# Value rows of the first gathered tile multiplied in the second half of the front, pair by pair

## The chip, the cores and the metric

The kernel runs on one core of a Trainium2 chip. The metric is the time of one execution on the device in microseconds (us), taken as the median of several runs. A profiled execution of the kernel gives the trace that the views below are read from.

## The reference

One layer of an encoder over 1024 tokens of width 1024, in float32. A combined projection feeds forgetting attention (FoX, 8 heads), an RWKV-7 scan (8 heads) and two merge gates; the merged result is normed into `x1`. Then comes PEER: each token picks experts by product keys and takes rows of two tables of 16384 experts.

```python
q = (xb @ w_q).reshape(t, PEER_HEADS, 2, PEER_HALF)
s = jnp.einsum('thpd,hpkd->thpk', q, sub_keys)
top_s, top_i = lax.top_k(s, K)                      # K = 16 on each side
...
best_s, best_pos = lax.top_k(cand_s.reshape(t, PEER_HEADS, K * K), K)
idx = jnp.take_along_axis(cand_i..., best_pos, axis=-1)   # 8 x 16 = 128 experts a token
gate = jax.nn.softmax(best_s, axis=-1)
h = gelu(einsum('thkd,td->thk', u_table[idx], xb))
out = einsum('thk,thkd->td', gate * h, v_table[idx])
```

The output is `layer_norm(alpha * x1 + out)`.

## The kernel before

The 1024 tokens are eight tiles of 128. **The front** runs twice, for 512 tokens each (`hf` 0 and 1): `fox` (attention), `rwkv_half` (the scan), `merge_half` (merge, output projection, norm) and `queries` (the 16 query projections and the scores of the keys). After it, `dense_block` treats the experts in two ways. Tiles 3, 4 and 5 (`DENSE`) are multiplied with all 16384 experts: a one-hot stage builds the matrix `C` of gates in 96 steps `k` (tile `ab` in, `v` out), then a loop of 128 steps `j` takes 128 experts each (`hidden`: tile `b` from `uh`, `ul`; `values`: tile `v` from `vh`, `vl`). Tiles 0, 1, 2, 6 and 7 (`GATHERED`) fetch the rows of their own experts by indirect DMA.

Two lists of small work are dealt out beside the main line. `g.B` (class `Background`) holds `topk` of each tile and `experts_in`: 128 gathers of `u` rows for a tile on the queue of GpSimd (POOL), each followed by one multiply-and-sum on VectorE (DVE). `g.V` holds `Rows.run`: for each gathered tile 64 **V steps**. A V step takes a pair of gathered value rows (two tiles of 128 x 1024, called `vr`, or `C` where places in `C` are lent) and multiplies each with a window of coefficients (`win`, one copy on ScalarE, ACT) in four float32 products into the PSUM bank `pg`. The trace has two records for each of the four, so a V step is eight records. `Rows.prepare` loads and turns the indices of a tile (`cij`, `ve`) first; `gather` asks for a pair of rows. A tile of `g.V` ends with `yd`, its result, written to DRAM; `finals` adds it to `x1` and norms.

What is dealt out is set at build time. `mm` adds up the nominal time of every product on the main line and calls `tick` of both lists; each tick adds time x `rate` to a credit, and steps are made while there is credit. A V step costs `VCOST` = 3.0, and in the loop two steps are made at a time. The rates are `RATEP` in the front, `RATEB[0]`, `RATEV[0]` in the one-hot stage, `RATEB[1]`, `RATEV[1]` in the loop and `RATEV[2]` once the keys of tile 7 are done. PE's instructions stand in the order in which the program makes them. In `dense_block` this holds for POOL and DVE too; elsewhere a scheduler orders the other engines. Each engine runs its own list in order.

In the scan, each group of 128 channels (`unit`) is a chain of small products with VectorE between them. At the points where the chain waits (`wait(us)`) a `Filler` puts in pieces of pending projections for `us` of nominal time; what is left is made at the unit's end (`F.drain`). In `merge_half` the products are `a`, `b` and `o`, in `queries` `o`; their weights come by DMA (`wh`, `wl` from `whd`).

Before the change `Rows` is made after the front, so that the first V step of tile 0 stands in the one-hot stage. Places for rows there are seven tiles `vr` and parts of `C` that are not yet used.

Of the kernel before, what the change touches and what calls it, by code (L numbers as in the profile page):

```python
# [20 lines left out]
T = 1024  # L21
# [8 lines left out]
RATEB = (2.1, 0.46)  # L30
RATEV = (4.2, 0.52, 1.25)
# [228 lines left out]
def build(tc, nc, A, dbg=None, stop=None):  # L260
    with ExitStack() as ctx:
# [4 lines left out]
        g.V.other = g.B  # L266
# [5 lines left out]
def mm(g, o, l, r, start, stop_):  # L272
    g.pe.matmul(o, l, r, start=start, stop=stop_)  # L273
# [127 lines left out]
def body(ctx, g):  # L401
# [19 lines left out]
    g.x1d = [dram(f"x1d{t}", (128, D)) for t in range(8)]  # L421
    g.scd = [dram(f"scd{t}", (128, 2048)) for t in range(8)]
# [13 lines left out]

    g.rank = g.tk.tile([128, 16, 16], BF16, name="rank")
# [29 lines left out]
    with ExitStack() as fe:  # L467
# [3 lines left out]
        for hf, (t0, n) in enumerate(PARTS):  # L471
            g.t0, g.n, g.cols = t0, n, slice(t0, t0 + n)
            with ExitStack() as hx:
# [9 lines left out]
                fox(g, hf, g.X)  # L483
                g.B.rate = RATEP[1]
# [4 lines left out]
                if g.stop not in ("fox", "rwkv"):  # L489
                    merge_half(g, hf, yr)  # L490
                g.keys.drop(more)
# [8 lines left out]
    g.psG = ctx.enter_context(tc.tile_pool(name="psG", bufs=1, space=PSUM))  # L500
    g.vx = ctx.enter_context(tc.tile_pool(name="vx", bufs=1))
    g.spare, g.over = True, False
    g.rows = Rows(g, GATHERED)
# [12 lines left out]
def front_setup(g, fe, order):  # L516
# [28 lines left out]
    g.ck = fp.tile([128, T], F32R, name="ck")  # L545
    dve.memset(g.ck.bitcast(F32), 0.0)
# [5 lines left out]
def fox(g, hf, X):  # L552
# [5 lines left out]
    ck = g.ck  # L558
    cols = g.cols
    with ExitStack() as fx:  # L560
        P = fx.enter_context(tc.tile_pool(name="fox", bufs=1))
        csel = P.tile([128, 8, 128], F32R, name="csel")
# [28 lines left out]
        with tc.tile_pool(name="fg", bufs=1) as fg, tc.tile_pool(name="xr", bufs=2) as xr:  # L591
# [21 lines left out]
            dve.scalar_tensor_tensor(ck[32:40, cols], cc, -1.0, ck[0:8, cols].bitcast(F32), op0=OP.mult, op1=OP.subtract)  # L613
            if "c" in g.dbg:
                sp.dma_start(g.dbg["c"][:, cols], cc)
# [43 lines left out]
        def chunks(ct, e, P_, yu, su, vc):  # L659
# [26 lines left out]
            yt = sm.tile([128, n], F32, name="th", bufs=4)  # L686
# [5 lines left out]
            if e:  # L692
# [4 lines left out]
                ri = sm.tile([128, n], F32, name="th", bufs=4)[0:2, :]  # L697
# [63 lines left out]
def rwkv_half(g, hf, X, kt):  # L761
# [12 lines left out]
    with ExitStack() as fx:  # L774
# [10 lines left out]
        psJ = fx.enter_context(tc.tile_pool(name="psJ", bufs=2, space=PSUM))  # L785
        psM = fx.enter_context(tc.tile_pool(name="psM", bufs=1, space=PSUM))
        psS = fx.enter_context(tc.tile_pool(name="psS", bufs=4, space=PSUM))

        def shifted(wt, out, ti):
            ps = psJ.tile([128, n], F32, name="pj")  # L790
            yield from proj_gen(g, ps, wt, X, 0)
            a = el.tile([128, n], F32, name="tmp", bufs=3)
# [6 lines left out]
        def gate(i):  # L799
            ps = psJ.tile([128, n], F32, name="pj")  # L800
            yield from proj_gen(g, ps, GATE + i, X, 0)
            t = el.tile([128, n], F32, name="tmp", bufs=3)
# [36 lines left out]
        for ct in range(5):  # L839
            if ct < 4:  # L840
                run(shifted(RW_K + ct, kt[:, ct, :], 2 + ct))
                sq = el.tile([128, n], F32, name="tmp", bufs=3)
# [96 lines left out]
        def unit(ct):  # L939
# [3 lines left out]
            def wait(us):  # L943
                F.fill(WAIT * us)
# [136 lines left out]
        g2 = el.tile([128, 512], F32, name="tmp", bufs=3)  # L1081
# [15 lines left out]
        F.fill(GN[0])  # L1097
        sums(psn, 3, sqs[3])
# [7 lines left out]
        F.fill(GN[1])  # L1106
        for ct in range(4):
            pr = psJ.tile([128, n], F32, name="pj")
# [17 lines left out]
def merge_half(g, hf, yr):  # L1126
# [3 lines left out]
    with ExitStack() as fx:  # L1130
# [4 lines left out]
        mt = mx.enter_context(tc.tile_pool(name="mt", bufs=2))  # L1135
        nt = n // 128
# [3 lines left out]
        with tc.tile_pool(name="psg", bufs=2, space=PSUM) as ps_:  # L1140
# [10 lines left out]
            for p, b in MERGE:  # L1151
                wm = g.W.get(W_MERGE + 2 * p + b)
                for dd in range(2):
# [7 lines left out]
                    if dd == 0:  # L1161
                        g.W.ahead()
                    dve.tensor_mul(t, t, pa)
# [17 lines left out]

        def turn(tts):
            for tt in tts:
                t = slice(tt * 128, (tt + 1) * 128)
                for k in range(0, 8, 4):
                    pt = ps_.tile([128, 4, 128], F32, name=f"o{(2 * tt + k // 4) % 4}", bufs=2)
# [19 lines left out]
        for m, tts in ((0, range(nt)), (1, range(half)), (1, range(half, nt))):  # L1206
            po = {tt: ps_.tile([128, 512], F32, name=f"o{tt}", bufs=2) for tt in tts}
            for k2 in range(4):
                w = g.W.get(W_OUT + 4 * m + k2)
                for kk in range(2):  # L1210
# [5 lines left out]
                    if kk == 0:  # L1216
                        g.W.ahead()
            for tt in tts:
# [7 lines left out]
        for later in rest:  # L1226
            later()
        mx.close()
        if g.stop != "merge":
            queries(g, hf, (x1h, x1l), lambda: turn(range(half, nt)), ps_)  # L1230
# [24 lines left out]
def queries(g, hf, x1, rest, ps_):  # L1255
# [5 lines left out]
    with ExitStack() as fx:  # L1261
# [3 lines left out]
        qs = {}  # L1265

        for i in range(2):
            w = g.W.get(W_Q + i)
            qs[i] = w, ps_.tile([128, n], F32, name=f"o{i}", bufs=2)
# [623 lines left out]
```

## Time and profile before

| what | us |
|---|---|
| median of three runs (lowest, highest) | 3612.66 (3611.28, 3629.97) |
| the profiled execution | 3579.33 |
| its span, first to last instruction | 3577.5 |

Busy time over the span, from the page: TensorE (PE) 3180.9 us (89%), its weight loads 2309.7 (65%), VectorE 2253.1 (63%), GpSimd 2066.4 (58%), ScalarE 1170.8 (33%). The DMA queues moved 1133.15 MB, 317 GB/s over the span. The second half of the front ends with the last product of the scores at 1776.5 us; the one-hot stage follows and the loop starts at 2212 us.

In the views, "busy" counts instructions that compute; a line's idle time is what its engine waited just before it, with the releaser behind "<-". PEclk is the clock that TensorE was granted, as a share of the full one. A DMA share of 1.00 means that all 16 DMA engines of the core were busy throughout.

### The profile page before, as it was taken

How to read it: one execution, taken by the hardware profiler on the slowest of the kernel's cores; microseconds unless marked ns; L12 is line 12 of the kernel's file. 1: busy time of each engine (PE TensorE's matmuls, PEld its weight loads, DVE VectorE, ACT ScalarE, POOL GpSimd, SP SyncE). 2: the span in 40 equal slices, each digit the busy share in tenths (PEclk: the TensorE clock that was granted, in tenths of full speed). 3: DMA queues.
4: the chain of work that ended last, by engine and by line, in shares of the span. 5: the costliest groups of instructions: out<-in, count | busy, mean ns of one | idle time of the engine just before them, and what ended most of it. 6: DMA issues, size and time to landing. Idle time of an engine off the chain costs nothing. (4 is left out here: it accounts for less than half of the span.)

```text
span 3577.5 us, 55699 instructions
## 1 busy us (share of the span) xinstructions
PE 3180.9 (89%) x20656; PEld 2309.7 (65%) x20656; DVE 2253.1 (63%) x5118; ACT 1170.8 (33%) x2453; POOL 2066.4 (58%) x1686
## 2 busy tenths in 40 slices
PE   7899998999998878788778866999999999999997
PEld 5577776786566656567533323877777777776675
DVE  2234533338988998887489854777666767774324
ACT  3442223333432221101144423333333333333332
POOL 2032114424655555663366566888887888886773
PEclk9899998999998987889889988999999999999998
DMA  6354336886979878999889999999999999999995
GB/s 223 115 184 152 116 136 246 287 314 246 328 276 378 302 272 295 369 333 386 314 348 393 373 370 368 365 360 361 389 392 378 398 385 399 397 394 341 400 400 190
DMA packets 369377, 1133.15 MB, mean 317 GB/s; under 512 B 49744, under 2 KB 88400, under 8 KB 367312
## 3 DMA queue, kind: packets, MB, share of 16 engines
q0 software_dynamic: 184320, 671.17, 49.1%
q1 hardware_dynamic: 172672, 437.64, 33.6%
q10 hardware_dynamic: 12112, 20.78, 1.6%
q8 instruction: 162, 2.65, 0.3%
q14 instruction: 111, 0.91, 0.1%
HBM read 999.87 MB, written 129.56 MB: 316 GB/s over the span
## 5 line engine op out<-in xcount | busy, mean ns | idle before, releaser
L1429 POOL DMA_INDIRECT g<-u,eidx x566 | 693.5, 1225 | 455.1 <-DVE hh L1435 160.9
L1435 DVE CUSTOM_DVE_ANT_0 g<-g,ext 128x1024 f32<-128x1024 f32 x566 | 723.6, 1288 | 75.3 <-DMA g<-u,eidx 75.1
L1731 POOL DMA_INDIRECT vr<-v,ve x434 | 459.8, 1059 | 187.6 <-issue 97.2
L291 POOL TENSOR_TENSOR wl<-wraw,wh 128x1024 fp32r<-128x1024 f32 x65 | 156.6, 2410 | 452.2 <-ACT wh L290 386.4
L273 PE MATMUL pg<-vr,win 128*32 128x512 f32 x1736 | 324.5, 630 | 76.1 <-DMA vr<-v,ve 76.0
L273 PE MATMUL b<-xh,uh 128*128 128x384 f32 x1024 | 349.9, 342 | 11.7 <-DVE C L1616 10.5
L273 PE MATMUL b<-xh,ul 128*128 128x384 f32 x1024 | 351.4, 343 | 5.1 <-POOL ul L291 4.9
L273 PE MATMUL b<-xl,uh 128*128 128x384 f32 x1024 | 349.0, 341 | 0.0
L273 PE MATMUL v<-vl,ch 128*128 128x512 f32 x768 | 304.7, 397 | 12.2 <-POOL vl L291 12.2
L273 PE MATMUL v<-vh,ch 128*128 128x512 f32 x768 | 302.5, 394 | 0.0
L273 PE MATMUL pj<-xh,wh 128*128 128x512 f32 x624 | 284.6, 456 | 20.1 <-DVE ql L586 8.6
L273 PE MATMUL v<-vh,cl 128*128 128x512 f32 x768 | 300.8, 392 | 0.0
L290 ACT CAST uh<-uraw 128x512 fp32r<-128x512 f32 x256 | 158.6, 620 | 362.6 <-PE b L273 334.6
L273 PE MATMUL pj<-xl,wh 128*128 128x512 f32 x624 | 260.3, 417 | 3.2 <-DVE xl L291 3.2
L273 PE MATMUL pj<-xh,wl 128*128 128x512 f32 x624 | 258.3, 414 | 0.0
L1731 POOL DMA_INDIRECT C<-v,ve x206 | 209.9, 1019 | 79.4 <-issue 50.5
L291 DVE TENSOR_TENSOR vl<-vraw,vh 128x512 fp32r<-128x512 f32 x128 | 134.3, 1049 | 183.8 <-ACT vh L290 175.2
L290 ACT CAST vh<-vraw 128x512 fp32r<-128x512 f32 x256 | 158.6, 621 | 257.8 <-PE v L273 214.9
L291 POOL TENSOR_TENSOR ul<-uraw,uh 128x512 fp32r<-128x512 f32 x128 | 170.6, 1333 | 85.7 <-ACT uh L290 75.8
L273 PEld LDWEIGHTS b<-xh,uh 128*128 128x128 f32 x1024 | 193.8, 189 | 32.7 <-DVE C L1616 12.6
L273 PEld LDWEIGHTS b<-xh,ul 128*128 128x128 f32 x1024 | 193.7, 189 | 32.2 <-issue 25.1
L273 PEld LDWEIGHTS b<-xl,uh 128*128 128x128 f32 x1024 | 193.9, 189 | 14.5 <-issue 10.1
(357 smaller groups left out, 6535.2 us busy)
## 6 DMA issues: line engine op xcount, KB each, us to landing
uraw<-ut SPq DMA_DIRECT2D x128, 512.0 KB, 6.7
vraw<-vt SPq DMA_DIRECT2D x128, 512.0 KB, 6.8
wraw<-w SPq DMA_DIRECT2D x75, 512.0 KB, 4.3
wh<-whd SPq DMA_DIRECT2D x75, 512.0 KB, 6.8
wl<-whd SPq DMA_DIRECT2D x75, 512.0 KB, 9.7
whd<-wh SPq DMA_DIRECT2D x71, 512.0 KB, 2.6
whd<-wl SPq DMA_DIRECT2D x71, 512.0 KB, 5.8
cd<-S SPq DMA_DIRECT2D x12, 1344.0 KB, 7.3
```

What stands on the lines that cost most here:

```text
L273: g.pe.matmul(o, l, r, start=start, stop=stop_)
L290: g.act.copy(hi, src)
L291: (lo_eng or g.dve).tensor_sub(lo, src, hi.bitcast(F32))
L1429: pool.indirect_dma_start(out=place, out_offset=None, in_=A["u"], in_offset=bass.IndirectOffsetOnAxis(ap=idx[:, n:n + 1], axis=0))
L1435: dve.tensor_tensor_reduce(out=gg, in0=gg, in1=xt, scale=1.0, scalar=0.0, op0=OP.mult, op1=OP.add, accum_out=hh[:, k:k + 1])
L1731: g.pool.indirect_dma_start(out=place, out_offset=None, in_=g.A["v"], in_offset=bass.IndirectOffsetOnAxis(ap=self.meta[i][1][:, t:t + 1], ...
```

## The change

`Rows` is made in the second half of the front, after `fox`. A V step becomes a method (`step`), and a new method `front` makes at most one thing each time it is called: a piece of `prepare`, a V step (when its rows were asked for at least 10 us ago and the last step is at least `gap` behind, both in nominal PE time), or one `gather` of a pair. It is called at the waits of a unit, twice behind the units, and in `merge_half` and `queries` behind each group of products. A step made in a unit takes 1.45 us off the filler of that wait. Rows have two places in the scan, two more in the merge and eight more in the queries; `leave` makes the steps that still hold a place before it goes. Steps made here do not tick the other lists.

To make room, `pg` takes a PSUM bank from the start of the second half's scan: there the projections share five banks `s` with the chain (before: four `s` and two `pj`), and bank `o3` of merge and queries has one buffer in place of two. The buffers `tmp` of the second half are two in place of three, `ck` is no longer kept across the halves but written to DRAM (`ckd`) and loaded again, and three small tiles of `fox` have buffers of their own. The rates change: `RATEB` from (2.1, 0.46) to (2.1, 0.575, 0.45, 0.45), `RATEV` from (4.2, 0.52, 1.25) to (3.7, 0.46, 0.44, 1.12); the third and fourth count from the end of the keys of tile 6 and of tile 7.

```diff
-RATEB = (2.1, 0.46)
-RATEV = (4.2, 0.52, 1.25)
+RATEB = (2.1, 0.575, 0.45, 0.45)
+RATEV = (3.7, 0.46, 0.44, 1.12)
+FRONT, MERGED, QUERIED = 2, 2, 8
+LAG, GAP, REST = 10.0, (14.0, 16.0), 3.0
...
 def mm(g, o, l, r, start, stop_):
...
+    g.now += us
     g.V.tick(us)
...
                 fox(g, hf, g.X)
+                if hf:
+                    g.psG = ctx.enter_context(tc.tile_pool(name="psG", bufs=1, space=PSUM))
+                    vp = hx.enter_context(tc.tile_pool(name="vf", bufs=1))
+                    g.vf = [vp.tile([128, D], F32, name=f"vr{i}") for i in range(FRONT)]
+                    g.rows = Rows(g, GATHERED)
+                    g.rows.places.add(g.vf)
...
-    g.rows = Rows(g, GATHERED)
     g.rows.places.add([g.vx.tile([128, D], F32, name=f"vr{i}") for i in range(RING)])
     g.V.add(g.rows.run())
...
-        psJ = fx.enter_context(tc.tile_pool(name="psJ", bufs=2, space=PSUM))
         psM = fx.enter_context(tc.tile_pool(name="psM", bufs=1, space=PSUM))
-        psS = fx.enter_context(tc.tile_pool(name="psS", bufs=4, space=PSUM))
+        psS = fx.enter_context(tc.tile_pool(name="psS", bufs=5 if hf else 4, space=PSUM))
+        psJ = psS if hf else fx.enter_context(tc.tile_pool(name="psJ", bufs=2, space=PSUM))
...
             def wait(us):
+                if hf and us >= 1.0:
+                    us -= g.rows.front(GAP[0])
                 F.fill(WAIT * us)
...
         F.fill(GN[0])
+        if hf:
+            g.rows.front(GAP[0])
...
                     if dd == 0:
                         g.W.ahead()
+                    if hf:
+                        g.rows.front(GAP[1])
                     dve.tensor_mul(t, t, pa)
...
                 act.copy(q[:, i % 4, :], ps)
+                if qv:
+                    g.rows.front(GAP[1])
...
-        if f"g{GATHERED[-1]}" in g.B.done:
-            g.V.rate = RATEV[2]
+        for i, t in enumerate(GATHERED[-2:]):
+            if f"g{t}" in g.B.done:
+                g.B.rate, g.V.rate = RATEB[2 + i], RATEV[2 + i]
...
+    def front(self, gap):
+        g = self.g
+        if self.prep:
+            if next(self.prep, 1):
+                self.prep = None
+        elif 0 not in self.meta:
+            if f"g{self.tiles[0]}" in g.B.done:
+                self.prep = self.prepare(0)
+                next(self.prep)
+        elif self.asked and g.now - self.asked[0] >= LAG and g.now - self.last >= gap:
+            self.asked.pop(0)
+            g.V.busy = True
+            self.step()
+            g.V.busy = False
+            self.last = g.now
+            return 1.45
+        elif self.ng < 128 and self.places.room(2) and g.now - self.last >= REST:
+            self.gather()
+            self.asked.append(g.now)
+        return 0.0
```

`step` is the body of the old loop of `run`, unchanged: one copy into `win`, four products into `pg`, and at the end of 32 pairs the result's copy and its two stores.

More of the change, by code (lines that the diff above doesn't have):

```diff
@@ L265, in build @@
         g.B, g.V = Background(tc), Background(tc)
-        g.V.other = g.B
+        g.V.other, g.now, g.rows = g.B, 0.0, None
         g.mx = ctx.enter_context(ExitStack())
@@ L490, in body @@
                     merge_half(g, hf, yr)
+                if hf and not g.stop:
+                    g.rows.leave(g.vf)
                 g.keys.drop(more)
@@ L1135, in merge_half @@
         mt = mx.enter_context(tc.tile_pool(name="mt", bufs=2))
+        mvs = []
+        if hf:
+            mv = mx.enter_context(tc.tile_pool(name="mv", bufs=1))
+            mvs = [mv.tile([128, D], F32, name=f"vr{i}") for i in range(MERGED)]
+            g.rows.places.add(mvs)
         nt = n // 128
@@ L1206, in merge_half @@
         for m, tts in ((0, range(nt)), (1, range(half)), (1, range(half, nt))):
-            po = {tt: ps_.tile([128, 512], F32, name=f"o{tt}", bufs=2) for tt in tts}
+            po = {tt: ps_.tile([128, 512], F32, name=f"o{tt}", bufs=nbuf(tt)) for tt in tts}
+            if mvs and tts.start:
+                g.rows.places.drop(mvs)
             for k2 in range(4):
@@ L1227, in merge_half @@
             later()
+        if mvs and not g.stop:
+            g.rows.leave(mvs)
         mx.close()
         if g.stop != "merge":
-            queries(g, hf, (x1h, x1l), lambda: turn(range(half, nt)), ps_)
+            queries(g, hf, (x1h, x1l), lambda: turn(range(half, nt)), ps_, nbuf)
 def layer_norm(g, mt, z):
@@ L1265, in queries @@
         qs = {}
+        qv = []
+        if hf and not g.stop:
+            qv = [qp.tile([128, D], F32, name=f"vr{i}") for i in range(QUERIED)]
+            g.rows.places.add(qv)
         for i in range(2):
             w = g.W.get(W_Q + i)
-            qs[i] = w, ps_.tile([128, n], F32, name=f"o{i}", bufs=2)
+            qs[i] = w, ps_.tile([128, n], F32, name=f"o{i}", bufs=nbuf(i))
             proj_part(g, qs[i][1][:, 0:h], w, x1, slice(0, h))
@@ L1286, in queries @@
             q = qp.tile([128, 4, n], F32, name="q", bufs=2)
+            if qv and gr == 3:
+                g.rows.places.drop(qv + g.vf)
             for i in range(4 * gr, 4 * gr + 4):
@@ L1300, in queries @@
         scores(*last)
+        if qv:
+            g.rows.leave(qv)
         for tt in range(n // 128):
@@ L1780, in leave @@
         while any(a is p for a in self.alive + self.held for p in places):
-            self.g.V._step()
+            if self.g.V.q:
+                self.g.V._step()
+            elif self.prep:
+                if next(self.prep, 1):
+                    self.prep = None
+            else:
+                self.asked.pop(0)
+                self.step()
+                self.last = self.g.now
         self.g.V.busy = False
```

117 lines of the change are left out of this document (69 added, 48 removed).

## The prediction

> **What bounds the kernel now.** First the page: the slices of TensorE, its clock and the DMA engines, and the queue of the gathers.
>
> ```profile
> PE   7899998999998878788778866999999999999997
> ...
> DMA  6354336886979878999889999999999999999995
> ...
> q0 software_dynamic: 184320, 671.17, 49.1%
> ```
>
> PE is busy without a break from the 26th slice on (the loop) and less so in the second half and the one-hot stage before it; the DMA engines stand at 8 or 9 tenths from the 17th slice to the end. q0 carries the 1280 gathers of rows (five tiles x 128, of `u` and of `v`): 671.17/1280 = 0.524 MB each, so a V step, a pair, costs 1.05 MB. Next, the windows by stage (busy of PE, PEld, DVE, ACT, POOL; then clock, DMA share, GB/s): scan of the second half, merge and queries, one-hot in two parts, loop in three.
>
> ```profile
> 1130.00:1520.00 390.00, 306.07 (x3799) 228.73 (x3799) 355.06 (x898) 77.84 (x131) 233.33 (x191) 0.84 0.87 315
> 1520.00:1787.00 267.00, 214.19 (x979) 173.88 (x979) 183.22 (x394) 38.50 (x69) 117.72 (x98) 0.90 0.90 346
> 1787.00:2050.00 263.00, 217.36 (x1172) 94.88 (x1172) 238.36 (x1095) 127.33 (x412) 157.12 (x158) 0.89 0.95 372
> 2050.00:2212.00 162.00, 109.25 (x535) 44.14 (x531) 85.98 (x267) 50.63 (x168) 112.54 (x100) 0.91 0.96 368
> 2212.00:2700.00 488.00, 474.67 (x2537) 378.37 (x2538) 327.11 (x555) 181.44 (x366) 397.93 (x329) 0.98 0.97 371
> 2700.00:3250.00 550.00, 532.73 (x2846) 423.61 (x2844) 384.13 (x499) 203.12 (x409) 463.41 (x381) 0.99 1.02 393
> 3250.00:3551.00 301.00, 293.35 (x1652) 209.48 (x1648) 84.05 (x119) 103.43 (x229) 198.51 (x186) 0.98 0.92 349
> ```
>
> PE idles 84 us in the scan, 53 in merge and queries, 98 in the one-hot stage (45.6 + 52.8) and only 38 in the loop, where it is the bound, with the DMA engines close behind. The same windows for the V steps alone (tile `pg`, eight records a step):
>
> ```profile
> 1787.00:2050.00 263.00, 136.09 (x624) 20.25 (x624) 1.17 (x2) 0.89 0.95 372
> 2050.00:2212.00 162.00, 71.19 (x276) 9.68 (x272) 0.59 (x1) 0.91 0.96 368
> 2212.00:2700.00 488.00, 66.74 (x528) 13.97 (x528) 1.17 (x2) 0.98 0.97 371
> ```
>
> In the loop a step takes 66.74/66 = 1.01 us, in the one-hot stage 1.74 to 2.06. The chain of waits shows what a `j` consists of:
>
> ```profile
> 2880.43 4.24 PE b L273 x24
> 2884.67 4.08 PE v L273 x18
> ```
>
> 4.24 + 4.08 = 8.32 us of dense work, and two V steps on top in two of three `j`. So each V step that leaves the loop is worth 1.0 us, without any cover. In the one-hot stage PE waits for the rows themselves (two rows of its waits, then the first gather on POOL and the first product):
>
> ```profile
> PE pg L273 <- DMA vr<-v,ve: 73.3, 53, 11.5
> PE pg L273 <- DMA C<-v,ve: 17.2, 13, 4.2
> ...
> 1798.42 0.95 POOL L1731 DMA_INDIRECT vr<-v,ve  x1 [25.11 <-DVE ve L1719]
> ...
> 1802.65 1.89 PE L273 MATMUL pg<-vr,win 128*32 128x512 f32 x2 [10.69 <-DMA vr<-v,ve]
> ```
>
> 90.5 us of waiting for some 112 steps, 10.69 of it at the start, since the indices are made only there.
>
> **The change, counted in PE's order.** Before, 0 V steps stand ahead of the first one-hot product, 112 in that stage, 208 behind it; after, 27, 102 and 191. So less than half of the first tile's 64 steps moves. The other edits of the rates move work inside the dense stages: the last step of the keys of tile 6 comes at `j` = 39 (before 49), of tile 7 at 95 (before 103).
>
> *Front: 27 steps added.* PE in the middle of a unit, before and after:
>
> ```order
> L273 MATMUL s<-Tm,M 64x64 x16
> L273 MATMUL pj<-xh,wh_84 128x512
> L273 MATMUL pj<-xl,wh_84 128x512
> L273 MATMUL pj<-xh,wl_85 128x512
> L273 MATMUL pj<-xh,wh_84 128x512
> L273 MATMUL pj<-xl,wh_84 128x512
> L273 MATMUL pj<-xh,wl_85 128x512
> L273 MATMUL s<-V,x 64x64 x16
> ```
>
> ```order
> L275 MATMUL s<-Tm,M 64x64 x16
> L275 MATMUL pg<-vr_8310,win 32x512
> L275 MATMUL pg<-vr_8309,win 32x512
> L275 MATMUL pg<-vr_8310,win 32x512
> L275 MATMUL pg<-vr_8309,win 32x512
> L275 MATMUL s<-V,x 64x64 x16
> ```
>
> The V step takes the place of six products of filler; those move to later waits, in the end into the steps of the state (`sigma`) that had none. So the step doesn't fill an empty place: the wait in front of it stays as long as before, and PE has about 1 us more to do unless the filler that moved finds idle time. 13 steps stand in units: 0 to 13 us, I take 8, since PE is idle 84 of 390 us there, but in few places. What waits in the scan and behind it (waits of PE in its two windows):
>
> ```profile
> PE s L273 <- DVE x L981: 28.8, 16, 4.8
> ...
> PE o L273 <- DMA wh<-whd: 18.4, 4, 8.9
> PE o L273 <- DMA wl<-whd: 8.6, 7, 2.0
> ...
> PE v L1496 <- DMA cij<-cijd: 7.5, 1, 7.5
> ```
>
> One step stands behind the units and ten in merge and queries. Placed on the times of before, three of these eleven meet a wait (one behind the units, two at late weights) and eight stand in dense projections: 8 x 1.0 = 8 us. The last three stand in the 7.5 us before `cij`: free. The DMAs of the 27 steps are 28 MB. In the scan, at 315 GB/s, they fit; around the queries they may not:
>
> ```profile
> 1600.00:1750.00 150.00, 0.00 (x0) 0.00 (x0) 0.00 (x0) 0.00 (x0) 0.91 1.00 395
> 1750.00:1787.00 37.00, 0.00 (x0) 0.00 (x0) 0.00 (x0) 0.00 (x0) 0.91 0.52 197
> ```
>
> Some 8 pairs are asked for between 1600 and 1750, 8.4 MB or 21 us at 395 GB/s, where the engines are full; the 37 us behind have room for 7 MB. Rows of `u` can be put off; weights can't. Nothing shows which gives way: 0 to 21 us, I take 4, near the low end, as PE has waited only 27 us for weights in all. Front: +20 us (0 to 42).
>
> The Trainium skill ("DMA: Bandwidth & Descriptors", section "SWDGE vs HWDGE vs iDMA") says that an engine's queues for software and hardware descriptors are served in turn. By that the weights keep their share, the 4 us would be 0 and the sum 4 us lower; the late weights above, at a share of 1.00, are no sign of it.
>
> *One-hot: ten steps fewer, and rows ready earlier.* PE at the start of the stage, before and after (`o` is the last score product, `ab` the one-hot tiles):
>
> ```order
> L273 MATMUL o_14133<-sk,q 128x128 x4
> L1496 MATMUL v_14186<-base,cij 128x128 x3
> L273 MATMUL v_14223<-ab 128x128 x4
> L273 MATMUL v_14243<-ab 128x128 x4
> L273 MATMUL v_14273<-ab 128x128 x3
> L1713 MATMUL b<-base,vr_14163 128x128 x3
> L273 MATMUL pg<-vr_14164,win 32x512
> ```
>
> ```order
> L1545 MATMUL v_14410<-base,cij 128x128 x3
> L275 MATMUL v_14447<-ab 128x128
> L275 MATMUL pg<-vr_14388,win 32x512
> L275 MATMUL pg<-vr_14389,win 32x512
> L275 MATMUL pg<-vr_14388,win 32x512
> L275 MATMUL pg<-vr_14389,win 32x512
> L275 MATMUL v_14447<-ab 128x128 x3
> ```
>
> The turn of the indices (`b<-base,vr`) is gone from the start; gathers can be issued as soon as the places are free. Two ways to price it. By PE: a step costs 1.74 to 2.06 us and 0.8 of waiting (90.5/112), so ten are 25 to 29 us. By DMA: 10.5 MB at 370 GB/s are 28 us, and a start some 10 us earlier comes on top. Against it stands DVE: busy 238 of the first 263 us, with work that stays, so that part can't shrink by more than 25. I take -27 us (-12 to -38).
>
> *Loop: 17 steps fewer.* 17 x 1.01 = -17 us. The loop lasts from 2212 to 3555, 1343 us; 128 x 8.32 + 208 x 1.01 = 1275 are work, 68 stalls. PE's idle time in the three windows is 13, 17 and 8 us, so they are spread. In the window with a DMA share of 1.02 fewer V steps and an earlier end of the keys take load off; ahead of it the keys come denser. I take -8 (-25 to +15). Loop: -25 us.
>
> *Tail.* DVE's last rows, before and after:
>
> ```order
> L1616 TENSOR_TENSOR C<-b,C 128x3x4x32
> L291 TENSOR_TENSOR cl<-C,ch 128x384
> L291 TENSOR_TENSOR vl<-vraw,vh 128x512
> L1797 SCALAR_TENSOR_TENSOR C<-C 128x512 x2
> L1238 BN_STATS st<-C 128x6 x2
> L1241 BN_AGGR mv<-st 128x2
> L1245 RECIPROCAL rs<-rs 128x1
> L1249 SCALAR_TENSOR_TENSOR C<-C,mv 128x1024
> L1250 SCALAR_TENSOR_TENSOR C<-C,rs 128x1024
> ```
>
> ```order
> L1887 SCALAR_TENSOR_TENSOR C<-C 128x512 x2
> L294 TENSOR_TENSOR ul<-uraw,uh 128x512
> L1665 TENSOR_TENSOR C<-b,C 128x3x4x32
> L294 TENSOR_TENSOR cl<-C,ch 128x384
> L1277 BN_STATS st<-C 128x6 x2
> L294 TENSOR_TENSOR vl<-vraw,vh 128x512
> L1280 BN_AGGR mv<-st 128x2
> ```
>
> The V steps end some two `j` earlier, and tile 7's norm goes in among the splits. Before, the last sums began behind it:
>
> ```profile
> 3554.84 0.39 PE L273 MATMUL v<-vh,cl 128*128 128x512 f32 x1
> ...
> 3556.81 1.28 DVE L1250 SCALAR_TENSOR_TENSOR C<-C,rs 128x1024 f32<-128x1024 f32 x1
> 3558.01 3.67 DVE L1797 SCALAR_TENSOR_TENSOR C<-C,v 128x512 f32<-128x512 f32 x6
> ```
>
> From the last product's end at 3555.2 to 3558.0: -2.5 us (0 to -2.8).
>
> *The small edits* (five banks for `s` in place of six, `tmp`, `o3`, `ck` by way of DRAM): a bank is written again only after products that need the same VectorE result; the load of `ck` is one of SP's transfers ahead of the second half, behind a short memset. Cover is the 5 us of every projection; without it a few us. I take 0 (-2 to +8).
>
> **Sum**: +20 - 27 - 25 - 2.5 = -34.5, so 3579.33 - 34.5 = 3544.8 us for the profiled execution. It lies 33 us under the median of the runs, 3612.66, and under all three; I carry the difference over: **3578 us**. A measurement here can tell about 0.5%, 18 us, from no change.
>
> **The rivals.**
>
> *The clock gains too.* After a long wait PE starts slowly:
>
> ```profile
> 1570.47 0.79 PE L273 MATMUL b<-xh,wh 128*128 128x512 f32 x1 [8.48 <-DVE g L1163]
> 1571.07 0.63 PE L273 MATMUL b<-xl,wh 128*128 128x512 f32 x1
> ```
>
> 0.60 us from start to start here, then 0.43 for about eleven products, where others of this form stand 0.23 apart: over 2 us for each such wait. The scan's clock is 0.84, 62 us lost of 390. If V steps and the filler behind them keep a third of that, and cost nothing in the units, the front gains 20 + 8 against the sum: -62 us, 3550. The Trainium skill's "TensorE: Matmul & The Clock Gate" (section "HAM oscillation — how this bites in real kernels") has the rule: an idle window of some 3.4 us halves the clock. The row agrees with it. Against: steps stand 14 us apart, and few stand in long waits.
>
> *The rows only move.* DMA engines are full from 1600 on and DVE holds the first part of the one-hot stage: front +36 (units 13, dense 8, DMA 15), one-hot -14, loop -17 without fewer stalls, tail -2.5: +2.5, so 3615, no change. For it: shares of 1.00 and DVE at 91%. Against: PE's 90 us of waits for rows.
>
> *The scan waits for its rows: slower.* PE runs in order, so a V step whose rows are late holds the chain. Gathers stand on POOL behind those of `u`, and these wait for DVE (waits of POOL in the scan):
>
> ```profile
> POOL g L1429 <- DVE hh L1435: 50.3, 34, 4.0
> ...
> POOL g L1429 <- DVE ti L1338: 17.6, 4, 16.1
> ```
>
> With the longest wait, 16.1, the 10 us of lead are gone. The sum without the units is -42.5; it is used up at 3.3 us for each of the 13 steps. At 5 us: +65 - 42.5 = +22, 3635. Against: most of POOL's waits are about 1.5 us.
>
> That the change doesn't do what it says is excluded for the places, which the order fixes; only 27 pairs is part of the sum.
>
> **How the numbers follow.** The forecast, -16 to -52: 0.52. The clock, beyond -52: 0.14. The rows only move, -16 to +15: 0.20. The scan waits, beyond +15: 0.14. Faster by over 18 us: all but a little of the first two, 0.65; within: 0.21; slower: 0.14. To leave out no more than 2 in 10 I cut at -62 (0.08 below) and at +20 (0.11 above): 3550 to 3633.
>
> **What would show it.** Front: the last score product at about 1797 (before 1776.5); the scan's length against 390 and any row "PE pg <- DMA vr" there tells the third rival. One-hot: from that product to the loop some 27 us less, and PE's waits for rows well under 90. Loop: 17 us less work and stalls under 68. Clock: over 0.84 in the scan speaks for the first rival. It would be wrong if the front grows by over 40 us, or the one-hot stage keeps its length.

## The result, and the profile after

| | median us | runs | ratio to before, 95% interval |
|---|---|---|---|
| before | 3612.66 (3596.74 to 3629.97) | 21 | |
| after | 3636.28 (3622.7 to 3654.29) | 21 | 1.0077 [1.0062, 1.0091] |

The kernel is slower by 0.8%. In two later groups of runs, each with the kernel before beside it on the same chip, the ratio was 1.0119 [1.0094, 1.0144] and 1.0061 [1.0038, 1.0084]. The forecast was 3578 us, faster.

From the page of the profiled execution after (span 3647.1 us): slices of PE and of the DMA engines, and the queue of the gathers.

```profile
PE   7899898999988877867966667899989999999997
...
DMA  6363246886889879889989889999999999999994
...
q0 software_dynamic: 184320, 671.17, 48.8%
```

The bytes are the same, 671.17 MB on q0; PE has a 6 in its 18th slice and in the 21st to the 24th, where before only the 24th and 25th had one. The windows by stage (busy of PE, PEld, DVE, ACT, POOL; then clock, DMA share, GB/s): scan, merge and queries, one-hot stage, loop in two parts.

```profile
1141.00:1580.70 439.70, 346.15 (x3917) 241.15 (x3918) 366.02 (x938) 85.39 (x156) 261.69 (x220) 0.82 0.86 312
1580.70:1888.00 307.30, 234.43 (x1080) 178.37 (x1078) 175.66 (x342) 40.24 (x79) 158.74 (x138) 0.88 0.96 372
1888.00:2293.00 405.00, 285.27 (x1622) 136.50 (x1622) 323.82 (x1360) 180.33 (x566) 230.02 (x221) 0.88 0.91 343
2293.00:3330.00 1037.00, 990.06 (x5239) 795.76 (x5238) 697.89 (x1058) 378.38 (x759) 838.81 (x684) 0.98 0.99 372
3330.00:3628.00 298.00, 297.16 (x1672) 220.61 (x1671) 91.90 (x125) 110.18 (x232) 189.95 (x177) 1.00 0.88 332
```

Cut at the same products as the windows before, to about 2 us, the scan with its norm lasts 440 us instead of 390, merge and queries 307 instead of 267, and the one-hot stage 405 instead of 425. What PE waits for between 1545 and 1895:

```profile
PE v L1545 <- DMA cij<-cijd: 17.3, 1, 17.3
PE b L275 <- DVE g L1193: 16.9, 4, 10.0
PE o L275 <- DMA wh<-whd: 14.7, 5, 4.3
PE o L275 <- DMA wl<-whd: 14.7, 8, 4.5
```

The wait for `cij`, 7.5 before, is 17.3; VectorE holds the merge for 16.9 us; the weights cost 29.4 (27.0 before). So the front ends 101 us later (1888 against 1787) and the dense stages are 31 us shorter, which makes the 70 us between the two spans.

### The profile page after: what moved, and what is told of

Same layout as the page of the kernel before. It is cut to its first block, busy times and chain, and to the rows that moved or that the text cites. A ratio compares the mean times of both kernels' runs of the same rounds, so it can differ in the third digit from the quotient of the medians.

```text
span 3647.1 us, 55678 instructions
## 1 busy us (share of the span) xinstructions
PE 3187.3 (87%) x20656; PEld 2329.4 (64%) x20656; DVE 2247.2 (62%) x5119; ACT 1180.3 (32%) x2458; POOL 2064.1 (57%) x1686
## 3 DMA queue, kind: packets, MB, share of 16 engines
q0 software_dynamic: 184320, 671.17, 48.8%
## 5 line engine op out<-in xcount | busy, mean ns | idle before, releaser
L1478 POOL DMA_INDIRECT g<-u,eidx x569 | 685.7, 1205 | 425.3 <-DVE hh L1484 133.4
L1783 POOL DMA_INDIRECT vr<-v,ve x444 | 483.0, 1088 | 255.3 <-issue 113.2
L275 PE MATMUL pg<-vr,win 128*32 128x512 f32 x1776 | 291.6, 639 | 41.6 <-DMA vr<-v,ve 38.0
L275 PEld LDWEIGHTS v<-ab 128*128 128x128 f32 x768 | 112.0, 216 | 184.6 <-issue 129.5
L294 DVE TENSOR_TENSOR vl<-vraw,vh 128x512 fp32r<-128x512 f32 x128 | 125.6, 981 | 159.2 <-ACT vh L293 94.7
L275 PE MATMUL v<-ab 128*128 128x128 f32 x768 | 140.2, 322 | 77.1 <-DVE ab L1561 48.1
L294 POOL TENSOR_TENSOR vl<-vraw,vh 128x512 fp32r<-128x512 f32 x128 | 178.8, 1397 | 38.0 <-ACT vh L293 35.4
```

The source lines that it names most:

```text
L294: (lo_eng or g.dve).tensor_sub(lo, src, hi.bitcast(F32))
L1478: pool.indirect_dma_start(out=place, out_offset=None, in_=A["u"], in_offset=bass.IndirectOffsetOnAxis(ap=idx[:, n:n + 1], axis=0))
L1783: g.pool.indirect_dma_start(out=place, out_offset=None, in_=g.A["v"], in_offset=bass.IndirectOffsetOnAxis(ap=self.meta[i][1][:, t:t + 1], ...
```

## The experiments

The kernels ran in groups, each on one chip beside the kernel before (the expectations say "call" for a group), and the level of the kernel before changed between groups: its medians were 3612.65, 3609.14, 3579.83, 3577.13 and 3574.98 us in groups 1 to 5. Ratios are therefore taken inside a group, and so are lengths of stages where that can be done; groups 2, 3 and 5 have no profile of before; before_again stands in for it in group 2, before_third in 3 and 5. The table gives the length of each stage in the profiled execution, cut at the same products in PE's order: "units" are the scan's four units, GN the norm behind them, "cij" the time from the last score product to the first one-hot product.

```
group kernel           to units units  GN  merge+out queries  cij  one-hot loop+tail   span
 1   before_again         1160   332  30.6   158       96    11.9    442    1381    3611.3
 1   room_only            1175   340  38.2   160       96    11.4    435    1381    3635.5
 1   after_again          1170   369  38.8   181      102    23.2    406    1362    3651.6
 1   old_rates            1179   370  38.8   178      103    23.3    427    1365    3685.3
 2   room_psum            1165   337  38.4   159       93    11.7    436    1383    3623.4
 2   room_rest            1161   338  37.2   157       95    11.4    436    1392    3628.6
 2   gathers_only         1171   358  38.8   176       93    23.0    404    1362    3624.9
 2   steps_no_rows        1156   339  42.5   159      103    24.1    405    1361    3590.1
 3   quarter_rows         1172   332  38.2   165      105    24.1    391    1355    3582.6
 3   loop_no_rows         1157   332  30.9   159       96    12.1    416    1372    3574.5
 3   loop_no_products     1154   338  32.8   155       97    11.9    416    1375    3580.4
 3   cij_early            1167   339  38.8   180      102    15.0    383    1360    3585.4
 4   before_third         1153   333  30.3   158       95    11.9    417    1374    3572.1
 4   after_third          1157   334  41.9   180      103    24.3    392    1356    3587.6
 4   cij_early_again      1173   335  38.8   180      102    16.0    383    1358    3586.2
 4   loop_neither         1157   337  31.3   155       97    11.7    418    1351    3560.3
 5   prep_only            1153   328  30.9   160       96    14.9    398    1379    3561.6
 5   scan_steps           1161   335  40.6   161       93    15.4    394    1393    3591.2
```

### Steps, room or rates

Theory A: the steps and their rows cost the front its time. Theory B: the room made for them does. Theory C: the new rates cost.

```diff
 room_only: rates of before, and
     def front(self, gap):
+        return 0.0
 old_rates: the kernel after with
+RATEB = (2.1, 0.46, 0.46, 0.46)
+RATEV = (4.2, 0.52, 0.52, 1.25)
```

> The kernel before, unchanged, for a second trace: the profiled execution of before took 3579 us, below every timed run of it. All theories expect 1.00 of the runs of before. If its stages stand as in the first trace (scan of the second half 370 us from 1130 to 1500, one-hot 425, loop 1343), the 100 us that the front of the changed kernel is longer are the change's; if the front alone differs by 20 us or more, the first trace was a lucky one and the cost of the front is that much smaller.

> The changed kernel, unchanged, for a second trace. All theories expect 1.008 (1.006 to 1.010) of the runs of before. Its front should again end 60 us or more behind that of before, with the one-hot stage and the loop 20 to 40 us shorter together.

> The changed kernel with the old rates and with no step, gather or preparation in the front: 0, 112 and 208 V steps as before, but the room made for them (five banks s, two tmp, one o3, a bank for pg, ck by way of DRAM). Theory A (the V steps and their rows cost the time in the front): 0.998 to 1.002 of before. Theory B (the room that was made for them costs it: fewer PSUM banks and buffers in the second half): 1.006 to 1.015, with the scan 20 us longer or more.

> The changed kernel with the rates of before: 27 V steps in the front, 115 in the one-hot stage, 178 in the loop (changed: 27, 102, 191). Theory A and B both put the loss in the front, which is the same here: 1.004 to 1.012. Theory C (the new rates cost time in the dense stages, the front is about even): 0.99 to 1.002.

Measured: before_again 1.0016 [1.0002, 1.003], room_only 1.0056 [1.0034, 1.0077], after_again 1.0119 [1.0094, 1.0144], old_rates 1.0187 [1.0158, 1.0216]. B holds for a part: the room alone, with no step in it, costs the front 31 us (1819.8 against 1788.3). Of these, 15 lie ahead of the units, where runs of the same instructions can differ as much (1157 in after_third, 1173 in cij_early_again). A holds for the rest: the front of the kernel after is 64 us longer still. C falls: old_rates lies above every forecast, and the new rates save 26 us. The first trace of the kernel before reaches its last score product when before_again does (1776.7 and 1777.0); it is shorter only behind it, by 24 us in the one-hot stage and 9 in the loop. So nothing was wrong with the front that was forecast from.

### Which room

room_psum is the kernel before with the bank edits alone (five banks `s` for the projections and the chain, one bank that nothing uses, `o3` single); room_rest has only the others (`tmp`, `ck`, `yt`, `ri`, the pools).

> The kernel before with only the bank edits in the second half: projections and scan on one set of five banks, one bank for the score products that nothing uses, the fourth output bank single. Theory 'banks' (the room's +31 us of the front come from fewer PSUM buffers): front 1788 -> about 1815, stages of chunks 4400-4800 and 6850-7445 longer by 9 and 15 us, ratio about 1.005. Theory 'memory' (they come from `tmp` with two buffers, `ck` through DRAM, `yt`/`ri` with one, and where the pools then lie): front 1788 to 1793, ratio 1.000 to 1.002.

> The other part of the room alone: `tmp`, `ck`, `yt`, `ri`, the pools for rows that nothing fills; banks as before. Theory 'banks': front 1788 to 1793, ratio 1.000 to 1.002. Theory 'memory': front about 1815, ratio about 1.005.

1.0025 [1.0, 1.0051] and 1.0031 [1.0008, 1.0054]: neither theory holds alone. The fronts are 1804 and 1800 us, so against before_again, on another chip, the parts cost 16 and 12 us, about half of the 31 each. Each by itself lengthens the norm GN by 7 us, as much as both together (7.6), so there the two do not add. PE's wait ahead of the merge's first product, in room_only, then in after_third:

```profile
PE a L275 <- issue: 6.4, 1, 6.4
```

```profile
PE a L275 <- issue: 10.6, 1, 10.6
```

It was 4.7 in before_third, put down to VectorE's `kt`; "issue" means that the profile shows nothing that PE waited for. In the kernel after, the norm also holds the step that stands behind the units and eleven product records of projections that the steps displaced; before_third has none of either there. Which buffer makes the norm longer was not taken apart.

### Products or rows

```diff
 gathers_only: step()
+        bare = not g.vx and 0 < m < 31
+        if not bare:
             g.act.copy(win[:, :, o:o + 1], c4[:, :, m:m + 1])
-        for h in range(2):
+        for h in range(0 if bare else 2):
 steps_no_rows: gather()
+            if g.vx or not any(p is place for p in self.seen):
                 g.pool.indirect_dma_start(out=place, ...)
 quarter_rows: gather(), from a place's second use on
+                in_=g.A["v"].rearrange("r (a c) -> (r a) c", a=4), out=place[:, 0:256]
```

> The kernel after, but of the 27 steps in the front only the first copies its window and multiplies; the other 26 fetch their rows and give the places back (these products are left out of the output). Theory 'products' (the steps' 65 us of the front are paid on TensorE and by ScalarE, which stands at the window's copy): front about 1830 instead of 1884, scan units 147 instead of 162, merge and output projection as in the kernel before, ratio about 1.00. Theory 'rows' (they are paid by the transfers: `u` rows that VectorE waits for, weights, `cij`): front 1870 to 1884, merge, output projection and `cij` wait as long as in the kernel after, ratio about 1.008.

> The kernel after, but a gather in the front is issued only the first time that a place is used (12 of 54 places); later steps multiply what lies there (their products are wrong rows). All 27 steps multiply as in the kernel after. Theory 'products': front 1870 to 1884, ratio about 1.010. Theory 'rows': front about 1830, VectorE's waits for gathered `u` rows in merge and queries back near 40 us from 88, `cij` wait near 12 us instead of 23, ratio about 1.00.

> The kernel after; each place's first gather in the front whole (12), the other 42 with a quarter of the bytes (1 KB a row instead of 4 KB, and other rows: their products are wrong). Same 54 gather instructions on the queue and on GpSimd. Theory 'bytes' (a step's rows cost their transfer: 1 MB at the 361 to 385 GB/s that the front's stages already move): three quarters of the 61 us come back, front about 1838, ratio about 1.000. Theory 'issue' (they cost by the number of gathers: queue turns, GpSimd's issue): front 1875 to 1884, ratio about 1.010.

gathers_only came out at 1.0055 [1.0032, 1.0077], steps_no_rows at 0.996 [0.9937, 0.9983], in one group: the whole loss is gone when 42 of the 54 gathers are not made, though all 27 steps multiply. The front of gathers_only, 1860, lies between its two theories. That of steps_no_rows (1823) is still 35 us longer than in before_again: 12 each in GN and in the gap before the first one-hot product, where the forecast of theory "rows" was missed (24.1 instead of 12), and 7 each in units and queries.

The stretch from the merge's first product to the last score product is the clearest. It lasts 256.0 us in before_again, 258.1 in room_only, 264.5 in steps_no_rows, 271.0 in gathers_only and 285.2 in after_again (groups 1 and 2, at nearly one level). So the steps without most of their rows cost 8.5 us, the rows without the products 15, both together 29, and 2 of each are the room's.

quarter_rows, with all gathers but a quarter of the bytes in 42 of them, had 0.9988 [0.9966, 1.001]. That ratio alone says little, since cij_early, with all the bytes, had 0.9994 in the same group. By the stages, against after_third, merge and output projection are at 165 instead of 180 us (158 before), so there it is mostly the bytes; the queries are at 105 (103), and the whole front is only 3 us shorter. Whether the number of gathers costs anything is not settled.

One way goes through VectorE. Its wait for gathered `u` rows between the norm and the one-hot stage, one row each from before_third, after_third, steps_no_rows, quarter_rows and scan_steps (below):

```profile
DVE g L1435 <- DMA g<-u,eidx: 41.2, 41, 2.7
```

```profile
DVE g L1484 <- DMA g<-u,eidx: 89.1, 54, 12.7
```

```profile
DVE g L1484 <- DMA g<-u,eidx: 47.4, 29, 14.1
```

```profile
DVE g L1484 <- DMA g<-u,eidx: 64.8, 42, 16.6
```

```profile
DVE g L1476 <- DMA g<-u,eidx: 42.2, 41, 3.1
```

Rows of `u` and of `v` share q0. With megabytes of `v` beside them, VectorE waits twice as long for `u` rows in all; the longest single wait is no sign of it, being longest in quarter_rows. VectorE runs in order and stands at the sum that needs the rows, and the merge's multiplication of `g`, which empties a bank for PE, stands behind it. PE's side of this, before_third, then after_third:

```profile
PE b L273 <- DVE g L1163: 7.4, 1, 7.4
```

```profile
PE b L275 <- DVE g L1193: 15.9, 5, 9.4
PE o L275 <- DMA wh<-whd: 14.0, 4, 4.5
PE o L275 <- DMA wl<-whd: 13.0, 7, 4.1
```

PE's waits for `g` are 8.5 us longer. That is not all that this stretch lost; before_third, then after_third:

```profile
1515.00:1770.40 255.40, 212.28 (x976) 172.52 (x976) 182.09 (x389) 35.67 (x61) 118.07 (x98) 0.92 0.93 361
```

```profile
1530.40:1815.90 285.50, 235.74 (x1060) 180.96 (x1064) 175.80 (x338) 37.17 (x70) 147.10 (x125) 0.89 0.96 370
```

PE idles 6.6 us more, so the waits explain only that much of the 30. It is busy 23.5 us more: 10.7 of them are the steps' own products (tile `pg`), and nearly 13 are the products of before taking longer, at a granted clock of 0.89 instead of 0.92. What slowed them was not isolated.

The weights, in another queue, cost 27.0 us, and 26.9 in before_third. The Trainium skill ("DMA: Bandwidth & Descriptors", section "Queues, rings and completion order") has each DMA engine turn from queue to queue; by that rule the weights keep their share beside the gathers, and these rows agree. The stores and the load of the next section, which SyncE issues as it does the weights, came late all the same.

### The load of cij

In the kernel after, `cij` lies in memory that the scores' last stores still read. The timeline of after_third (start, duration):

```profile
1812.33 0.94 POOL L1783 DMA_INDIRECT vr<-v,ve  x1 [19.35 <-PE o L275]
...
1813.86 9.29 SPq L1325 DMA_DIRECT2D scd<-sc  x4
...
1829.50 0.32 SPq L1541 DMA_DIRECT2D cij<-cijd  x1
...
1836.32 0.87 PE L1545 MATMUL v<-base,cij 128*128 128x128 f32 x3 [17.71 <-DMA cij<-cijd]
```

and of before_third:

```profile
1768.39 4.47 SPq L1282 DMA_DIRECT2D scd<-sc  x4
...
1775.08 0.32 SPq L1492 DMA_DIRECT2D cij<-cijd  x1
1777.86 0.88 PE L1496 MATMUL v<-base,cij 128*128 128x128 f32 x3 [7.43 <-DMA cij<-cijd]
```

With the indices ready, 16 gathers of the next stage are issued between 1812.33 and 1831.19, the first two ahead of the four small stores and the others among and behind them; the stores land late, SyncE waits for them, and `cij` is issued 6.4 us behind them instead of 2.2, and lands 6.8 us later instead of 2.8. cij_early puts it into a place of the rows, so that it is issued first.

```diff
-        cij = bp.tile([128, 3, 128], F32, name="cij", bufs=1)
+        if i:
+            cij = bp.tile([128, 3, 128], F32, name="cij", bufs=1)
+        else:
+            p = g.rows.places.take()
+            cij = p[:, 0:384].rearrange("p (a b) -> p a b", a=3)
         sp.dma_start(cij, g.cijd[tiles[i]])
```

> The kernel after, with the first `cij` of the one-hot stage loaded into a place of the rows instead of memory that the scores' stores still read, so that SyncE issues it ahead of the last four `scd` stores. If the 23 us between the last score product and the first one-hot product are its late issue (1874.92, behind stores that lie in the transfers of the next stage's first 16 gathers), they fall to 5 to 12 us and the time by about 12 to 15, ratio about 1.007. If the load only waits in another place (the transfers are full at 400 GB/s), they stay above 18.

> The kernel before, beside the three below on one chip. Over the calls so far its median was 3609 to 3613 and 3580 us and its one-hot stage 418 and 442 us long: if that is the chip, the stages of all four here stand at one level; ratio 1.000.

> The kernel after on the same chip as the next. Theory 'the front pays the rows in transfer time': front longer than that of before by 70 to 100 us, dense stages shorter by 40 to 62; ratio 1.003 (a chip that moves more bytes) to 1.012.

> As `cij_early`. Theory 'late issue': 8 to 15 us less than the kernel after in this call, all of it between the last score product and the first one-hot product; units of the scan as in the kernel after. Theory 'chip': its ratio of 0.9994 came from the chip, and `after_third` stands within 4 us of it.

cij_early was at 0.9994 [0.9974, 1.0015], which by itself said nothing, since that group was 30 us faster as a whole. Beside after_third (1.0061) it was 1.0021 [1.0002, 1.004], 11 us less by the medians. In the profiled executions the gap is 8.3 us shorter and the one-hot stage 8 us; the spans differ by only 1.4, since 16 us are lost ahead of the units (1173 against 1157), where both run the same instructions. Theory "late issue" holds by the time and by the gap, though not all of the gain lies in the gap, as it had said; 4 us of the longer gap remain.

### What the dense stages gained by

Three versions of the kernel before, in which 27 steps of the dense stages (10 and 17, as many as the change took away) lose their rows, their products, or both:

```diff
+FEWER = set(range(33, 43)) | set(range(121, 189, 4))
```

> The kernel before, with the rows of 27 steps not fetched (10 in the one-hot stage, 17 in the loop; places seen before only); the products run on what lies there. It says what in the dense stages a moved step sets free. Theory 'bytes' (the dense stages gained 55 to 62 us because 27 MB left them): one-hot stage and loop together shorter by 45 to 60, ratio about 0.985. Theory 'products' (as forecast: PE work and waits of the loop): shorter by 0 to 15, ratio 0.996 to 1.000.

> The kernel before, with the window copy and the products of the same 27 steps left out and their rows still fetched (part of the output is missing). Theory 'products': one-hot stage and loop shorter by 35 to 60, ratio 0.984 to 0.990. Theory 'bytes': shorter by 0 to 20, ratio 0.995 to 1.000.

> The kernel before without the rows and without the products of the same 27 steps of the dense stages (left out alone, each gave 0.1 to 0.2%). Theory 'two full engines' (TensorE busy 0.97 and the DMA engines 0.98 to 1.00 in the loop, either hides what the other saves): one-hot stage and loop shorter by 40 to 60 us, ratio 0.984 to 0.990. Theory 'order' (what the kernel after gains there comes from earlier keys and rates, not from fewer steps): shorter by 0 to 15, ratio 0.996 to 1.000.

0.998 [0.9958, 1.0002], 0.9989 [0.997, 1.0009] and 0.9931 [0.9908, 0.9955]. Rows or products alone buy at most 0.2%. Both buy 0.7%, which lies between the two theories of loop_neither, and they buy it in the loop. The windows of the loop, one from each: before_third, loop_no_rows, loop_no_products, loop_neither.

```profile
2198.30:3550.00 1351.70, 1308.22 (x7064) 1012.27 (x7062) 807.75 (x1187) 492.17 (x1013) 1070.15 (x898) 0.99 0.98 373
```

```profile
2202.70:3552.40 1349.70, 1309.71 (x7064) 1015.72 (x7062) 771.47 (x1186) 493.12 (x1013) 1033.66 (x867) 0.99 0.96 362
```

```profile
2205.50:3558.30 1352.80, 1300.16 (x6928) 1015.62 (x6926) 809.36 (x1187) 488.52 (x996) 1060.50 (x897) 0.98 0.98 373
```

```profile
2208.90:3538.20 1329.30, 1289.49 (x6928) 1007.13 (x6926) 799.45 (x1186) 489.20 (x996) 1028.94 (x867) 0.99 0.97 367
```

Two resources are nearly full together: PE is busy for 0.97 of the loop before, and the DMA engines have a share of 0.98. Without the products PE is busy 8 us less and idles 9 us more (52.6 instead of 43.5), at the same 373 GB/s; without the rows PE is busy as long as before. Only when both go, the loop is 22 us shorter, 1.3 us a step. The one-hot stage, 418 us, gained nothing from the ten steps. There VectorE took over; PE's wait in loop_neither:

```profile
PE v L274 <- DVE ab L1513: 29.2, 13, 4.0
```

In before_third this wait was 2.4 us. So the 25 us that the kernel after gains there come from something else, which the next run tests.

### Two that might be faster

prep_only is the kernel before, with the indices of the first tile made ready in the queries and the early `cij`: no step in the front, no room, rates of before. scan_steps is cij_early with front steps in the units only, and with the rates of before in the loop.

```diff
 prep_only: queries(), second half
+            cj0 = qp.tile([128, 3, 128], F32, name="cj0")
+            sp.dma_start(cj0, g.cijd[GATHERED[0]])
...
+            if hf and gr == 1 and not g.stop:
+                g.meta0 = turned_in(g, 0, cj0, ps_.tile([128, 4, 128], F32, name="o3", bufs=2))
```

`turned_in` is the second half of `prepare`: three transposes, two copies, two operations on VectorE.

> The kernel before, with only the indices of the first gathered tile made ready during the queries (one cij load, three transposes, two copies, two VectorE operations, 1 KB of memory) and with the early cij load; no room for rows, no step in the front, the rates of before; 115 steps in the one-hot stage and 205 in the loop. Theory 'start' (the one-hot stage of the kernel after gained its first-half 11 to 17 us by rows that were on their way 27 us before the first one-hot product, not by having fewer steps): front 1776 to 1785, first half of the one-hot stage 5 to 15 us shorter, ratio 0.993 to 0.998. Theory 'fewer steps': no gain but the cij load's, ratio 0.998 to 1.001.

> cij_early with front steps in the scan only (and what is left of the last rows when they leave): 14 in the front, 102 in the one-hot stage, 204 in the loop, the loop's rates of before; the places in merge and queries are gone. On a chip like that of after_third the merge, output projection and queries lose their 29 us and the scan costs 0: front 1800 to 1815, one-hot stage near 385, loop 4 to 8 us shorter than before, ratio 0.993 to 1.000. If the places and the room, not the steps, cost merge and queries, the front stays near 1840 and the ratio at 1.003 to 1.010.

prep_only: 3563.04 us, 0.9957 [0.9934, 0.9981], faster than the kernel before beside it. Its gathers of `v` start at 1766.42 (in before_third at 1792.1). The gap before the first one-hot product is no shorter for that, 14.9 us against 11.9: `cij` is there early (its products write `v` from a place `vr`), but the copy of their result on ScalarE stands behind score stores that land late.

```profile
1776.30 0.90 PE L1507 MATMUL v<-base,vr 128*128 128x128 f32 x3 [6.62 <-ACT sc L1286]
...
1781.13 0.48 ACT L1508 COPY cT<-v 128x384 f32<-128x384 f32 x1 [4.88 <-DMA scd<-sc]
...
1783.42 0.79 PE L273 MATMUL v<-ab 128*128 128x128 f32 x2 [6.21 <-DVE ab L1525]
```

The one-hot stage, with three more steps in it, is 18 us shorter (398.2 against 416.6). Its two halves, prep_only, then before_third:

```profile
1784.00:1961.40 177.40, 152.22 (x869) 67.23 (x869) 167.98 (x777) 91.17 (x298) 118.30 (x119) 0.93 1.01 398
1961.40:2182.20 220.80, 165.88 (x840) 68.18 (x840) 152.55 (x573) 83.60 (x275) 145.05 (x136) 0.90 0.99 383
```

```profile
1781.70:1972.70 191.00, 157.08 (x848) 67.91 (x848) 170.99 (x788) 92.22 (x301) 119.06 (x120) 0.91 0.94 370
1972.70:2198.30 225.60, 162.69 (x841) 67.96 (x841) 150.92 (x564) 83.23 (x275) 144.47 (x136) 0.90 0.97 376
```

The DMA engines go from a share of 0.94 to 1.01 in the first half: rows that start earlier fill a gap that no step has to be moved for. Theory "start" holds: an earlier start, without fewer steps, is worth some 18 of the 25 us by these two traces. What part of the 18 is due to the early `cij`, which this run has too, was not separated; in cij_early_again it went with 8 us less in this stage. scan_steps, 1.0051 [1.0028, 1.0074], missed its forecast, though its front did what was expected (1805; merge, output projection and queries back at 254 us, as in before_third, and VectorE's wait for `u` at 42.2). Its loop and tail are 19 us longer than in before_third with four steps fewer, which was not expected and stays open.

## Why the prediction was wrong

**The step that failed is the front's +20 us (0 to 42).** In group 4 it measured +58 (1839.6 against 1781.7), in group 1 +96; over 40 was what the prediction itself named as the sign of being wrong. By its terms, in group 4:

- *13 steps in the units, 8 us.* +0.3 in group 4 (333.5 against 333.2), +37 in group 1 (369.4 against 332.0); room alone is +8. The steps' own products take the same time in both (16.1 and 15.8 us of tile `pg`). What differs is told in the last section; its cause stays open. The third rival's mechanism was not seen: no product in the units waits for its rows.
- *Eight steps in merge and queries, 8 us, and their DMAs, 4 of 0 to 21.* Measured +30 together (283 against 253 in merge, output projection and queries), and +1 without the steps and places there (scan_steps). The 8 us were right: steps without most of their rows cost 8.5 (steps_no_rows). The term for the DMAs was too small: rows without products cost 15 (gathers_only), and 22 of the 30 are more than the steps' 8, just past the end of the range; the value was chosen near the low end because nothing showed what gives way. It named the rows of `u` as what could be put off. They gave way, and it was not free: VectorE, in order, carried the delay to PE, for some 8 us; the products that ran longer, nearly 13 us, were no term of the sum.
- *Three last steps free in the wait for `cij`.* The gap went from 11.9 to 24.3. The sum never asked what the prepared indices would set off: 16 gathers around the stores that `cij` waits for.
- *Small edits, 0 (-2 to +8).* +31 in the front of room_only, 12 to 16 for each half, of which GN and the units have 8 each and 15 lie ahead of the units, where they may be chance. In group 4 GN is 11.6 longer, and 3.5 of the +58 lie ahead of the units. The cover named, 5 us in each projection, is not there in the norm, which in room_only has no product of a projection.

**One-hot -27 and loop with tail -27.5** measured -25.0 and -17.4 in group 4, -36.5 and -18.9 in group 1. The loop's 17 us came out (17 x 1.01), the 8 us of stalls did not; but the reason given, PE's work without any cover, was half of it, since the same products alone bought nothing (loop_no_products). The one-hot size was right by luck in part: ten steps fewer give nothing there (loop_neither), an earlier start gives some 18 (prep_only). PE's waits for `vr` rows in that stage fell from 70.9 to 39.6 in group 4, as forecast, but VectorE's `ab` took over part of it. What gives the other 7 us was not isolated; old_rates, 21 us longer there than after_again with 13 steps more, points to the rates.

**Sum of group 4**: +57.9 - 25.0 - 17.4 = +15.5, the difference of the spans. **The rivals**: "the rows only move" had the right idea, with 15 us for transfers and nothing for the room. "The scan waits for its rows" had the right time by a mechanism that did not act. "The clock gains too" is out as a time: over scan and norm the clock was 0.82 in the first trace after. Its mechanism does show in group 4, where the units ran at 0.90 with the steps and 0.87 without, and 13 steps cost 0.3 us.

**The first trace** of the kernel before, 33 us under its median, resembles groups 3 to 5 in its one-hot stage (418 us; 442 in before_again). Carrying the difference over was harmless; the sum was wrong, not the scale.

## What to carry to other kernels

When work is moved, move its transfers in the sum too. Here the DMA engines stood at 0.9 or more in merge and queries and behind them, and in merge and queries the rows alone cost 15 us, the products alone 8.5. Ask what shares their queue, which in-order engine waits for it, and what stands behind that. In a stage with two nearly full resources, price the relief of both together: one alone gained 2 us or nothing in the loop here, both 22. Before moving work, try moving only what lets it start: here two loads and a few small operations gave 0.4%, where the whole change cost 0.8%.

## What the runs showed of the hardware

The level of one kernel differed between groups, and the traces show where, though not why. Windows of the one-hot stage of the kernel before, before_again (group 1), then before_third (group 4):

```profile
1788.30:2230.60 442.30, 313.29 (x1687) 140.46 (x1687) 320.88 (x1351) 172.15 (x575) 262.59 (x255) 0.85 0.92 351
```

```profile
1781.70:2198.30 416.60, 319.76 (x1687) 135.88 (x1687) 321.91 (x1351) 175.45 (x575) 263.53 (x255) 0.91 0.96 373
```

That is 26 us in one stage, more than the 24 us between the medians of the result. The bytes are the same, 155 MB, and the DMA engines' share is lower in the longer stage, so the lower GB/s is the longer time seen from another side and no proof of slower DMA engines. PE's waits for rows are shorter there, too (55.5 us for `vr` against 69.9, and 15.0 for `C` in before_third alone). What before_third does not have at all are these two rows of before_again:

```profile
PE v L273 <- issue: 28.4, 16, 5.0
PE v L273 <- remote: 11.5, 2, 5.8
```

For both, the profile shows no instruction that PE waited for. In the units with the steps it is alike; after_again, then after_third:

```profile
1169.90:1539.30 369.40, 292.17 (x3617) 208.82 (x3614) 305.78 (x770) 68.18 (x127) 224.21 (x186) 0.86 0.85 304
PE s L275 <- issue: 16.7, 37, 1.2
```

```profile
1156.90:1490.40 333.50, 269.12 (x3616) 194.29 (x3613) 307.32 (x772) 68.19 (x127) 223.30 (x187) 0.90 0.90 336
```

Of the 36 us between them, 23 are longer busy time of the same products at a lower granted clock, and 13 are idle time. Waits of the kind "issue" stand in the units and in the one-hot stage of every trace of groups 1 and 2 and of the first trace after, and in none of groups 3 to 5 nor in the first trace before. What makes them was not found. Groups 1 and 3 had the same chip, so it is not the chip alone. The Trainium skill ("DMA: Bandwidth & Descriptors", section "Measured (HBM→SBUF, 128 partitions, SWDGE, issued from GpSimd)") gives a core about half of its memory's rate while its neighbour streams too; no run here shows whether a neighbour was busy.
